# First feed-forward of a decoder block: four plain tiles in place of six, chunks of 6, 8 and 8

## The chip, the cores and the metric

The kernel runs on one core of a Trainium2 chip (trn2). The metric is the device time of one execution in microseconds (us). Five engines work side by side, each through its own queue in order: PE (TensorE, matrix products; PEld its weight loads), DVE (VectorE), ACT (ScalarE), POOL (GpSimd) and SP (SyncE, which issues nearly all transfers).

## What is computed

One decoder block on 528 tokens (16 learned meta tokens ahead of 512) with 1024 channels, in fp32: a SwiGLU feed-forward, a token mixer (latent attention beside a gated DeltaNet), a second SwiGLU feed-forward, a final norm. The change touches the first feed-forward alone:

```python
def swiglu(x, w_gate, w_up, w_down):
    return (jax.nn.silu(x @ w_gate) * (x @ w_up)) @ w_down

h = h + 0.5 * swiglu(rmsnorm(h, ffn1_norm[l]), ffn1_w_gate[l], ffn1_w_up[l], ffn1_w_down[l])
```

`w_gate` and `w_up` are 1024 x 2816, `w_down` is 2816 x 1024. The hidden size of 2816 is 22 tiles of 128.

## The kernel before, in words

Activations lie with channels on the 128 partitions and tokens along the row: `hk`, eight tiles of 128 x 528. Each fp32 product is made of three fast ones: an operand is split into a rounded high part (ACT casts it) and the remainder (DVE subtracts), and high x high, high x low and low x high are added up in PSUM. So each weight tile costs a cast on ACT and a subtraction on DVE before PE can use it.

A feed-forward is the function `ffn`, called for both. Its 22 hidden tiles `ft` go in chunks (`CHUNKS1`, `CHUNKS2`). The first `2 * nc_` tiles are **plain** (`NC1 = 3` in the first feed-forward, `NC2 = 2` in the second): for gate and for up, `weights` loads and splits a 128 x 1024 weight (L175 to L177), `mm3` (L204) runs 8 x 3 x 2 matmuls of 264 columns, the result is multiplied by the norm's `r` (L390; for the first two tiles L376 and L386), and gate and up are joined (L400). Such a product (gate or up of one tile) is called a unit here: six plain tiles are twelve units of 48 matmuls.

The other tiles go by twos through `quad` (L440), a scheme of Strassen and Winograd on a 2 x 2 split of weights, channels and tokens: 7 products instead of 8. Each product is 12 matmuls of 264 columns, so a quad is 84, and two tiles take two quads (gate, up). In exchange DVE and ACT have more to do: in a quad, DVE makes four sums of weights (`side`, L429, tiles `sf`), the low halves of seven weight forms (`form`, L292; ACT casts the high halves, L291) and seven sums of results from PSUM (L433); ACT copies one result (L456). DVE joins the two tiles at L495.

A quad also needs the activations in another form, which DVE and ACT build once per feed-forward while PE is busy with the plain tiles: for each of four pairs of `hk` tiles two scalings by `r` (L407), four differences (L413) and splits (L291, L292) into tiles `hd` (named `b`, `yh`, `yl` in the code) and `ut` (`sh`, `sl`, `th`, `tl`). The scaling needs `r`, thus the norm of the whole input.

When a chunk's tiles are done, each is split (`halve`, L292 `hd<-hd,ra`), and `down` (L204 `dn`, L345) multiplies the chunk by eight blocks of `w_down`; these eight calls are spread over the quads of the chunk behind it, and the last chunk's eight stand at the end. A `down` of 8 tiles is 48 matmuls, of 6 tiles 36.

```python
for ft in range(2 * nc_):                       # plain tiles
for c, (k0, k1) in enumerate(CHUNKS):
    nq = max(k1 - max(k0, 2 * nc_), 0)
    for ft in range(max(k0, 2 * nc_), k1, 2):
        for j in range(2):
            quad(ft, j, *os)
            if c:
                while given < KT * q // nq:
                    down(c - 1, given)
    for ft in range(k0, k1):
        halve(ft)
for m in range(KT):
    down(len(CHUNKS) - 1, m)
```

The order on each engine is not this program order: a scheduler sorts the instructions when the program is built, and each engine then takes its own queue strictly as it stands. The weight tiles rotate through a few buffers, and the forms through three kinds in turn (`CYCLE`, counted over both feed-forwards).

Of the kernel before, what the change touches and what calls it, by code (L numbers as in the profile page):

```python
# [51 lines left out]
M34 = 17.5  # L52
WLO = ()
LAG = 3
NC1 = 3
NC2 = 2
CHUNKS1 = ((0, 8), (8, 16), (16, 22))
CHUNKS2 = ((0, 6), (6, 14), (14, 22))
BANKS = "smastsa"
NG = 3  # L60
# [35 lines left out]
def build(tc, a, out, tap=None):  # L96
# [3 lines left out]
    with ctx:  # L100
# [202 lines left out]
        def ffn(wg, wd, xs, hks, wname, r, n, hid, tmp, ra, rb, hk_tile, nc_, load, finish, pre=()):  # L303
            raws, hs, hkm = [], {}, {}
            pre = list(pre)
            h = n // 2
            CHUNKS = CHUNKS1 if n == NT else CHUNKS2

# [201 lines left out]
        with tc.tile_pool(name="hid", bufs=1) as hid, tc.tile_pool(name="fp", bufs=2) as fp:  # L510
# [61 lines left out]

            ffn(a["w1"], a["d1"], xs, hks, "n1", r, NT, hid, fp, ra1, upt, hk1, NC1, load1, finish1, pre)
            r = norm2.finish(D, "r")
# [984 lines left out]
```

## Time and profile before

| | |
|---|---|
| median of 3 runs | 1169.24 us (1168.03 to 1169.33) |
| profiled execution | 1168.86 us, its span 1167.1 us |
| PE busy | 1152.7 us, 99% of the span |
| DVE busy | 859.5 us, 74% |
| ACT busy | 560.3 us, 48% |
| chain that ended last | PE 94%; DVE 2%; ACT 2%; DMA 1% |
| granted TensorE clock, mean | 0.998 of full speed |

The profile is of one execution; times in it count from the start of its span. A row of the timeline shows the start, the time from the first start to the last end in it, the engine, the line, the operation and the tiles. Rows of one engine overlap a little, since an instruction begins before the one ahead of it has written its last value: the pace of a queue is the distance from start to start, not the duration. This holds for PE above all, where a matmul of 264 columns is shown with 0.28 us and the next one starts 0.12 us after it.

### The profile page before, as it was taken

To read this page: it belongs to the slowest core of one execution; us is meant where nothing else is said; L and a number is where in the kernel's file an instruction comes from. 1 tells how busy PE (TensorE), PEld (TensorE's weight loads), DVE (VectorE), ACT (ScalarE), POOL (GpSimd) and SP (SyncE) were. 2 spreads that over 40 slices of the span, in tenths; PEclk is the share of its full clock that TensorE was granted. 3 is DMA by queue.
4 is the path that set the end of the run, shared out by engine and by line. 5 is a ranking of instruction groups with operands and counts; after the bars stand their busy time and mean duration, and the time that the engine had idled before them with its cause. 6 is when DMAs were issued, how large, how long until landed. Compare 5 with 4: busy or idle time off the path is not lost.

```text
span 1167.1 us, 20801 instructions
## 1 busy us (share of the span) xinstructions
PE 1152.7 (99%) x8132; PEld 1053.9 (90%) x8132; DVE 859.5 (74%) x1588; ACT 560.3 (48%) x989; POOL 83.0 (7%) x108
## 2 busy tenths in 40 slices
PE   9999999999999999999999999999999999999997
PEld 9999999999999989888877888878899999999986
DVE  6998787776665879963786666645999878877744
ACT  7554343533445584365466554434454445433443
POOL 0000000000003221001100000221000000000011
PEclk9999999999999999999999999999999999999999
DMA  6432332333235433445656445555433333323322
GB/s 243 129 124 96 109 104 97 95 94 103 82 101 174 153 89 122 138 148 154 186 157 180 136 131 167 184 178 174 155 105 132 111 93 105 101 100 107 93 71 73
DMA packets 74114, 148.51 MB, mean 127 GB/s; under 512 B 20288, under 2 KB 30864, under 8 KB 74016
## 3 DMA queue, kind: packets, MB, share of 16 engines
q1 hardware_dynamic: 73472, 146.66, 39.9%
q8 instruction: 64, 1.05, 0.4%
q10 hardware_dynamic: 544, 0.52, 0.1%
q14 instruction: 34, 0.28, 0.1%
HBM read 128.56 MB, written 18.60 MB: 126 GB/s over the span
## 4 chain that ended last, share of the span: by engine, by line
PE 94%; DVE 2%; ACT 2%; DMA 1%; issue 1%; SPq 0%; DVEq 0%; ACTq 0%
PE gu L440 30%; PE dn L204 21%; PE gu L204 10%; PE gate L204 8%; PE wo L204 4%; PE mo L204 4%; PE qkv L204 3%; PE z L204 2%; PE s L1169 2%; PE cq L204 1%; ACT dec L150 1%; PE pt L1202 1%; PE o L1231 1%; PE qk L1025 1%; PE vn L996 1%; PE qn L204 1%
## 5 line engine op out<-in xcount | busy, mean ns | idle before, releaser
L176 ACT CAST whi<-wraw 128x1024 fp32r<-128x1024 f32 (+2 forms) x121 | 122.9, 1016 | 174.1 <-issue 66.4
L177 DVE TENSOR_TENSOR wlo<-wraw,whi 128x1024 fp32r<-128x1024 f32 (+2 forms) x121 | 146.5, 1211 | 24.6 <-ACT whi L176 24.4
L440 PE MATMUL gu<-hd,form 128*128 128x256 f32 (+1 forms) x1224 | 164.7, 283 | 0.0
L440 PEld LDWEIGHTS gu<-hd,form 128*128 128x128 f32 x1224 | 155.9, 190 | 1.6
L291 ACT CAST form<-sf 128x512 fp32r<-128x512 f32 x136 | 83.0, 620 | 113.9 <-DVE sf L429 65.7
L440 PE MATMUL gu<-rb,form 128*128 128x256 f32 x864 | 112.6, 283 | 0.0
L345 DVE SCALAR_TENSOR_TENSOR hk<-dn,hk 128x528 f32<-128x528 f32 (+2 forms) x50 | 33.9, 678 | 100.7 <-PE dn L204 100.7
L440 PEld LDWEIGHTS gu<-rb,form 128*128 128x128 f32 x864 | 107.7, 192 | 0.0
L291 ACT CAST form<-wraw 128x512 fp32r<-128x512 f32 x102 | 63.1, 620 | 85.9 <-PE gu L440 56.4
L292 DVE TENSOR_TENSOR form<-sf,form 128x512 fp32r<-128x512 f32 x136 | 92.8, 688 | 12.3 <-ACT form L291 12.1
L440 PE MATMUL gu<-ut,form 128*128 128x264 f32 x768 | 101.1, 284 | 0.0
L204 PE MATMUL dn<-hd,whi 128*128 128x264 f32 (+2 forms) x376 | 99.0, 315 | 0.0
L440 PEld LDWEIGHTS gu<-ut,form 128*128 128x128 f32 x768 | 96.5, 188 | 0.0
L204 PE MATMUL gate<-ut,whi 128*128 128x512 f32 x256 | 86.5, 412 | 1.3 <-DVE gt L1259 1.3
L204 PE MATMUL dn<-ut,whi 128*128 128x512 f32 (+1 forms) x248 | 85.4, 381 | 0.0
L204 PE MATMUL dn<-ra,whi 128*128 128x264 f32 x464 | 85.3, 285 | 0.0
L292 DVE TENSOR_TENSOR form<-wraw,form 128x512 fp32r<-128x512 f32 x102 | 69.8, 687 | 6.4 <-ACT form L291 6.0
L204 PE MATMUL dn<-ut,wlo 128*128 128x512 f32 (+1 forms) x192 | 72.1, 375 | 0.0
L204 PE MATMUL dn<-ra,wlo 128*128 128x264 f32 x352 | 71.6, 285 | 0.0
L204 PEld LDWEIGHTS dn<-ra,whi 128*128 128x128 f32 x464 | 68.5, 189 | 0.0
L204 PEld LDWEIGHTS dn<-hd,whi 128*128 128x128 f32 x376 | 62.9, 189 | 3.9
L204 PE MATMUL qkv<-ut,whi 128*128 128x264 f32 x384 | 65.2, 288 | 0.0
(434 smaller groups left out, 2311.5 us busy)
## 6 DMA issues: line engine op xcount, KB each, us to landing
wraw<-w SPq DMA_DIRECT2D x86, 512.0 KB, 3.3
wraw<-win SPq DMA_DIRECT2D x36, 512.0 KB, 3.5
wraw<-d SPq DMA_DIRECT2D x32, 512.0 KB, 3.7
wraw<-d SPq DMA_DIRECT2D x16, 384.0 KB, 3.2
hk<-xT SPq DMA_DIRECT2D x16, 264.0 KB, 4.4
dec<-growd SPq DMA_DIRECT2D x8, 512.0 KB, 6.2
gated<-gt SPq DMA_DIRECT2D x16, 256.0 KB, 2.0
sg<-gated SPq DMA_DIRECT2D x16, 256.0 KB, 2.9
```

Of the source, the lines that this page charges most:

```text
L150: ins = nc.scalar.activation(*args, **kw).ins
L176: ih = nc.scalar.copy(hi[:, 0:n], raw[:, 0:n])
L177: il = (nc.gpsimd if pool_lo else nc.vector).tensor_tensor(out=lo[:, 0:n], in0=raw[:, 0:n], in1=hi[:, 0:n].bitcast(F32), op=ALU.subtract)
L204: trail.append(nc.tensor.matmul(o, lhsT=w, rhs=x[:, lo_:hi_], start=start and k == 0 and pi == 0, stop=stop and k == n - 1 and pi == 2).ins)
L291: nc.scalar.copy(hi, x)
L292: (eng or nc.vector).tensor_tensor(out=lo, in0=x, in1=hi.bitcast(F32), op=ALU.subtract)
L345: nc.vector.scalar_tensor_tensor(out=o, in0=p, scalar=0.5, in1=o, op0=ALU.mult, op1=ALU.add)
L440: nc.tensor.matmul(ps, lhsT=wt, rhs=xt, start=k == 0 and i == 0, stop=k == 3 and i == 2)
L996: nc.tensor.matmul(psv[:, h], lhsT=X[c][:, h], rhs=rr[:, h], start=True, stop=True)
L1025: nc.tensor.matmul(ps[:, h4], lhsT=hs(kT, h, o, o + n), rhs=hs(qT, h, o, o + n), start=True, stop=True)
L1169: nc.tensor.matmul(ps[:, 0:w], lhsT=Q[h][:, b * P:(b + 1) * P], rhs=K[h][:, k0:k1], start=True, stop=True)
L1202: nc.tensor.transpose(out=ps[:, b * P:(b + 1) * P], in_=Pr[h // 2, b][:, h % 2, NM + c * P:NM + (c + 1) * P], identity=ident)
```

## The change

The first feed-forward takes the numbers that the second one has: four plain tiles in place of six, and chunks of 6, 8 and 8 tiles in place of 8, 8 and 6.

```diff
-NC1 = 3
+NC1 = 2
 NC2 = 2
-CHUNKS1 = ((0, 8), (8, 16), (16, 22))
+CHUNKS1 = ((0, 6), (6, 14), (14, 22))
 CHUNKS2 = ((0, 6), (6, 14), (14, 22))
```

So tiles 4 and 5 go through two quads in place of four units; chunk 0 has four plain tiles and two quads (before: six and two), chunk 1 has eight quads, now with calls of `down` of 6 tiles between them (before: 8), chunk 2 has eight quads (before: six) with calls of 8 tiles (as before), and the eight calls at the end have 8 tiles (before: 6).

What the queues look like is shown at three places, as rows of line, operation, output, inputs and shape; numbers behind a name tell buffers apart.

**DVE, at the third plain tile's end.** The two queues are the same up to the first row here. `wlo` is the low part of a plain unit's weight, `hk` and `hd`, `ut` the activations for the quads. Before:

```order
L400 TENSOR_TENSOR hd_455<-g_454,hd_455 128x528
L177 TENSOR_TENSOR wlo_691<-wraw_689,whi_690 128x1024
L413 TENSOR_TENSOR hk_110<-hk_110 128x264
L407 SCALAR_TENSOR_TENSOR hk_111<-hk_111,cols_74,r_213 128x528
L413 TENSOR_TENSOR hk_110<-hk_114,hk_110 128x264
L407 SCALAR_TENSOR_TENSOR hk_115<-hk_115,cols_74,r_213 128x528
L413 TENSOR_TENSOR hk_114<-hk_114,hk_110 128x264
L292 TENSOR_TENSOR ut_953<-hk_110,ut_952 128x528
L390 TENSOR_TENSOR g_570<-gu_572,r_213 128x528
L413 TENSOR_TENSOR hk_114<-hk_114 128x264
L177 TENSOR_TENSOR wlo_748<-wraw_746,whi_747 128x1024
```

With the change:

```order
L400 TENSOR_TENSOR hd_455<-g_454,hd_455 128x528
L413 TENSOR_TENSOR hk_110<-hk_110 128x264
L407 SCALAR_TENSOR_TENSOR hk_111<-hk_111,cols_74,r_213 128x528
L413 TENSOR_TENSOR hk_110<-hk_114,hk_110 128x264
L407 SCALAR_TENSOR_TENSOR hk_115<-hk_115,cols_74,r_213 128x528
L413 TENSOR_TENSOR hk_114<-hk_114,hk_110 128x264
L292 TENSOR_TENSOR ut_721<-hk_110,ut_720 128x528
L413 TENSOR_TENSOR hk_114<-hk_114 128x264
L292 TENSOR_TENSOR hd_730<-hk_111,hd_730 128x264
L292 TENSOR_TENSOR hd_732<-hk_115,hd_731 128x528
L390 TENSOR_TENSOR g_570<-gu_572,r_213 128x528
L292 TENSOR_TENSOR ut_723<-hk_114,ut_722 128x528
```

The weight splits `wlo` of tiles 4 and 5 (691, 748 and two more) have gone from the queue, and with them the results of these tiles; what is left moves up.

**DVE, the first weight forms.** The last rows of the activations and the forms of the first quad. Before:

```order
L292 TENSOR_TENSOR ut_995<-hk_112,ut_994 128x528
L413 TENSOR_TENSOR hk_116<-hk_116 128x264
L429 TENSOR_TENSOR sf_1031<-sf_1029,wraw_1006 128x512
L429 TENSOR_TENSOR sf_1067<-wraw_1006,wraw_1007 128x512
L292 TENSOR_TENSOR ut_997<-hk_116,ut_996 128x528
L390 TENSOR_TENSOR hd_687<-gu_745,r_213 128x528
L292 TENSOR_TENSOR form_1013<-wraw_1006,form_1013 128x512
L400 TENSOR_TENSOR hd_687<-g_686,hd_687 128x528
L292 TENSOR_TENSOR form_1034<-sf_1031,form_1034 128x512
```

With the change:

```order
L400 TENSOR_TENSOR hd_571<-g_570,hd_571 128x528
L413 TENSOR_TENSOR hk_112<-hk_112 128x264
L292 TENSOR_TENSOR form_781<-wraw_774,form_781 128x512
L413 TENSOR_TENSOR hk_112<-hk_116,hk_112 128x264
L429 TENSOR_TENSOR sf_797<-wraw_775 128x512
L413 TENSOR_TENSOR hk_116<-hk_116,hk_112 128x264
L292 TENSOR_TENSOR ut_763<-hk_112,ut_762 128x528
L413 TENSOR_TENSOR hk_116<-hk_116 128x264
L429 TENSOR_TENSOR sf_799<-sf_797,wraw_774 128x512
L292 TENSOR_TENSOR form_819<-wraw_774,form_819 128x512
L292 TENSOR_TENSOR ut_765<-hk_116,ut_764 128x528
L292 TENSOR_TENSOR form_802<-sf_799,form_802 128x512
```

Before, `form_1013` (the first quad's first product) stands behind `hd_687`, the result of the tenth of twelve units; now `form_781` (the same product) stands right behind `hd_571`, the result of the eighth and last unit, and `form_819` and `form_802` (its third and second product) follow.

**PE, from the last plain unit to the first quad.** `gu` are the PSUM tiles; the first row is the last plain matmul pair. Before:

```order
L204 MATMUL gu_861<-ra_171,wlo_864 128x264 x2
L440 MATMUL gu_1012<-hd_920,form_1013 128x264 x3
L440 MATMUL gu_1012<-hd_941,form_1013 128x264 x3
L440 MATMUL gu_1012<-hd_962,form_1013 128x264 x3
L440 MATMUL gu_1012<-hd_983,form_1013 128x264 x3
L440 MATMUL gu_1033<-ut_933,form_1034 128x264
```

With the change:

```order
L204 MATMUL gu_629<-ra_171,wlo_632 128x264 x2
L440 MATMUL gu_780<-hd_688,form_781 128x264 x2
L440 MATMUL gu_818<-hd_689,form_819 128x264
L440 MATMUL gu_818<-hd_690,form_819 128x264
L440 MATMUL gu_780<-hd_688,form_781 128x264
L440 MATMUL gu_780<-hd_709,form_781 128x264 x3
L440 MATMUL gu_780<-hd_730,form_781 128x264 x3
L440 MATMUL gu_780<-hd_751,form_781 128x264 x3
L440 MATMUL gu_818<-hd_689,form_819 128x264
L440 MATMUL gu_801<-ut_701,form_802 128x264
L440 MATMUL gu_801<-ut_702,form_802 128x264
L440 MATMUL gu_818<-hd_710,form_819 128x264
```

Before, a product's twelve matmuls stand together. Now two matmuls of the third product (`gu_818`) are put between the second and the third one of the first product (`gu_780`); the third matmul of each is the first that reads the low half of its form.

**DVE, the first forms of chunk 1.** The splits of chunk 0's tiles (`hd<-hd,ra`), the joins of its last two tiles (L495), and the forms of chunk 1's first quad: `form_1321`, `form_1342`, `form_1359` before, `form_1081`, `form_1119` with the change. Before:

```order
L292 TENSOR_TENSOR hd_1295<-hd_687,ra_1294 128x528
L429 TENSOR_TENSOR sf_1337<-wraw_1315 128x512
L292 TENSOR_TENSOR hd_1299<-hd_803,ra_1298 128x528
L429 TENSOR_TENSOR sf_1339<-sf_1337,wraw_1314 128x512
L433 TENSOR_TENSOR cp_1146<-gu_1169,p1_1147 128x264
L292 TENSOR_TENSOR form_1359<-wraw_1314,form_1359 128x512
L292 TENSOR_TENSOR form_1321<-wraw_1314,form_1321 128x512
L433 TENSOR_TENSOR hd_1004<-gu_1186,p1_1147 128x264
L292 TENSOR_TENSOR form_1342<-sf_1339,form_1342 128x512
```

With the change:

```order
L292 TENSOR_TENSOR hd_1055<-hd_455,ra_1054 128x528
L433 TENSOR_TENSOR hd_772<-gu_1010,cp_914 128x264
L292 TENSOR_TENSOR hd_1059<-hd_571,ra_1058 128x528
L495 TENSOR_TENSOR hd_772<-hd_772,g_770 128x528
L433 TENSOR_TENSOR hd_773<-gu_1027,cp_914 128x264
L292 TENSOR_TENSOR form_1081<-wraw_1074,form_1081 128x512
L495 TENSOR_TENSOR hd_773<-hd_773,g_771 128x528
L292 TENSOR_TENSOR hd_1063<-hd_772,ra_1062 128x528
L429 TENSOR_TENSOR sf_1097<-wraw_1075 128x512
L292 TENSOR_TENSOR hd_1067<-hd_773,ra_1066 128x528
L429 TENSOR_TENSOR sf_1099<-sf_1097,wraw_1074 128x512
L292 TENSOR_TENSOR form_1119<-wraw_1074,form_1119 128x512
```

Before, three forms of this quad stand ahead of the joins (which come 11 rows below the last row shown) and of the splits of the last two tiles; now `form_1081` stands behind a join and the last splits of plain tiles, and `form_1119` behind both joins and all six splits.

## Rows read from the trace of the kernel before

**Rows 1.** The page, part 1: busy time, share of the span, instructions.

```profile
PE 1152.7 (99%) x8132; PEld 1053.9 (90%) x8132; DVE 859.5 (74%) x1588; ACT 560.3 (48%) x989; POOL 83.0 (7%) x108
```

**Rows 2.** Waits of PE over the whole span: total us, times, longest.

```profile
PE gu L204 <- ACT whi L190: 1.3, 1, 1.3
```

**Rows 3.** Windows of the first feed-forward: busy time by engine, clock, DMA.

```profile
core 0: us, PE busy (x) PEld busy (x) DVE busy (x) ACT busy (x) POOL busy (x), PEclk, DMA share, GB/s
...
78.13:108.73 30.60, 30.60 (x255) 30.60 (x253) 30.38 (x58) 16.00 (x29) 0.00 (x0) 1.00 0.33 104
108.73:205.17 96.44, 96.44 (x795) 96.44 (x793) 73.06 (x130) 38.34 (x62) 0.00 (x0) 1.00 0.31 99
```

**Rows 4.** Timeline of PE: start, us, operation, count in the row.

```profile
54.98 0.65 PE L204 MATMUL gu<-ra,whi 128*128 128x264 f32 x4
...
78.13 1.62 PE L440 MATMUL gu<-hd,form 128*128 128x264 f32 x12
...
108.73 0.40 PE L204 MATMUL dn<-ra,whi 128*128 128x264 f32 x2
```

**Rows 5.** Timeline of DVE, norm and first rows behind it.

```profile
29.42 0.43 DVE L225 SCALAR_TENSOR_TENSOR r<-rsq,r 128x264 f32<-128x264 f32 x1
...
35.87 1.45 DVE L407 SCALAR_TENSOR_TENSOR hk<-hk,cols,r 128x528 f32<-128x528 f32 x2
...
45.48 0.71 DVE L400 TENSOR_TENSOR hd<-g,hd 128x528 f32<-128x528 f32 x1
```

**Rows 6.** Timeline of DVE, consecutive rows, for the pace of each kind.

```profile
54.26 0.78 DVE L407 SCALAR_TENSOR_TENSOR hk<-hk,cols,r 128x528 f32<-128x528 f32 x1
54.94 0.45 DVE L413 TENSOR_TENSOR hk<-hk 128x264 f32<-128x264 f32 x1
...
61.22 0.45 DVE L413 TENSOR_TENSOR hk<-hk 128x264 f32<-128x264 f32 x1
61.56 0.71 DVE L292 TENSOR_TENSOR form<-wraw,form 128x512 fp32r<-128x512 f32 x1
62.16 0.72 DVE L390 TENSOR_TENSOR g<-gu,r 128x528 f32<-128x528 f32 x1
62.78 1.24 DVE L177 TENSOR_TENSOR wlo<-wraw,whi 128x1024 fp32r<-128x1024 f32 x1
63.91 0.45 DVE L413 TENSOR_TENSOR hk<-hk 128x264 f32<-128x264 f32 x1
...
68.60 0.71 DVE L292 TENSOR_TENSOR form<-wraw,form 128x512 fp32r<-128x512 f32 x1
...
106.45 0.43 DVE L433 TENSOR_TENSOR cp<-gu,cp 128x264 f32<-128x264 f32 x1
106.79 0.69 DVE L429 TENSOR_TENSOR sf<-sf,wraw 128x512 f32<-128x512 f32 x1
```

**Rows 7.** Timeline of DVE in the second feed-forward: first scaling, first forms.

```profile
816.05 0.75 DVE L407 SCALAR_TENSOR_TENSOR hk<-hk,cols,r 128x512 f32<-128x512 f32 x1
...
842.91 0.69 DVE L292 TENSOR_TENSOR form<-wraw,form 128x512 fp32r<-128x512 f32 x1
...
848.16 0.69 DVE L292 TENSOR_TENSOR form<-sf,form 128x512 fp32r<-128x512 f32 x1
```

**Rows 8.** Timeline of PE in the second feed-forward: first product of its first quad.

```profile
850.75 1.59 PE L440 MATMUL gu<-hd,form 128*128 128x256 f32 x12
```

**Rows 9.** Windows at the end of the span, columns as in rows 3.

```profile
1158.50:1159.00 0.50, 0.12 (x1) 0.00 (x0) 0.00 (x0) 0.34 (x1) 0.00 (x0) 1.00 0.00 0
...
1161.50:1162.00 0.50, 0.00 (x0) 0.00 (x0) 0.50 (x2) 0.00 (x0) 0.00 (x0) 0.72 0.00 0
1162.00:1162.50 0.50, 0.00 (x0) 0.00 (x0) 0.50 (x2) 0.00 (x0) 0.00 (x0) 0.50 0.00 0
```

**Rows 10.** Timeline of DVE in the last calls of `down`, first feed-forward.

```profile
348.70 0.71 DVE L345 SCALAR_TENSOR_TENSOR hk<-dn,hk 128x528 f32<-128x528 f32 x1 [2.08 <-PE dn L204]
349.37 0.96 DVE L177 TENSOR_TENSOR wlo<-wraw,whi 128x768 fp32r<-128x768 f32 x1
```

## The prediction

> **What bounds the kernel now.** I read the page first, then the waits, then windows and timelines of the first feed-forward. PE is busy for 99% of the span [rows 1], and in the whole span the longest wait of PE is one of 1.3 us, at the start [rows 2]. So PE's own queue is the time: each matmul less counts, as long as the other engines keep ahead, and each wait that a change brings to PE counts in full. The reader should then look at how far ahead DVE is. While the two quads of chunk 0 and the first of chunk 1 run, DVE is busy for 30.38 of 30.60 us; with the calls of `down` between the quads, for 73.06 of 96.44 us [rows 3]. So DVE has no spare time just at the stretch that the change makes earlier.
>
> **The gain on PE.** Four plain units, 192 matmuls, take from 54.98 to 78.13 us, 23.15 us; three quads, 252 matmuls, take 30.60 us up to 108.73 us, 10.20 us each or 0.1214 us a matmul [rows 4]. Tiles 4 and 5 go from four units to two quads: 20.40 − 23.15 = **−2.75 us**.
>
> **What comes earlier.** PE is done with the eighth unit at 54.98 us [rows 4]. Up to there its queue is the same as before. Before, it then had four more units, and DVE and ACT had these 23 us for the activations and the first forms. Now the first quad follows at once. The activations can't start earlier: the last half of `r` is written from 29.42 us on, and the first scaling starts at 35.87 us [rows 5].
>
> **DVE's queue, counted out.** The paces, start to start [rows 6]: a scaling L407 0.68 us; a difference or split of 264 columns 0.34; a form or weight sum of 512 columns 0.60; an operation on 528 columns 0.62; a `wlo` 1.13; a sum from PSUM (L433) 0.34. Up to L400 at 45.48 us [rows 5] the two queues are the same, so the next row starts at 46.10. Between it and `form_781` there now stand 24 rows: 11 of 264 columns (3.74), 4 scalings (2.72), 9 of 528 columns (5.58), together 12.04 us. The result of the eighth unit is among them; PE has it by 55.3, DVE comes to it at about 55.9, so DVE does not wait there. `form_781` starts at 58.14 and ends 0.71 us later [rows 6], at 58.85.
>
> - **First wait.** PE issues four matmuls (54.98 to 55.47) and stands at the first that reads the low half of `form_781`: 58.85 − 55.47 = 3.38 us. Ten matmuls follow (1.21), to 60.06.
> - **Second wait.** `form_819` starts seven rows behind `form_781` (3 × 0.60 + 3 × 0.34 + 0.62 = 3.44), at 61.58, and ends at 62.29: 2.23 us. `form_802` starts at 61.58 + 0.60 + 0.62 = 62.80 and ends at 63.51, ten matmuls later, just when PE needs it.
> - **Third and fourth wait.** From `form_802` to `form_1081` there are 37 rows: 18 of 512 columns (10.80), 14 sums (4.76), 5 of 528 (3.10), 18.66 us. So `form_1081` starts at 81.46 and ends at 82.17. PE has 154 matmuls of the two quads left at 62.29 (18.70) and four of the third: 81.48. Wait 0.69 us; ten matmuls, 83.38. `form_1119` starts six rows on (0.60 × 3 + 0.62 × 3 = 3.66) at 85.12 and ends at 85.83: wait 2.45 us.
>
> Together 3.38 + 2.23 + 0.69 + 2.45 = **+8.75 us**. Behind that the rest of this quad (8.5 us) reads forms that DVE makes at 0.60 us each, and the first `down` gives DVE 4.3 us of PE time for one `wlo` and one sum.
>
> **The other edits, at nothing.** ACT casts 28 half forms in place of 4 weights; it is busy for 16.00 of 30.60 us there [rows 3], and each cast it owes DVE stands one or more rows ahead. The transfers are the same in number and size; SP now issues the eight reloads of `hk` ahead of chunk 1's first weights, but they wait for the same DVE rows as the first quad from about 63 us on, and have some 15 us until `form_1081`. In chunk 1 a quad with a `down` of 6 tiles gives PE 10.20 + 36 × 0.1206 = 14.5 us, and DVE needs what it needs now, 73.06/6 = 12.2 us for each of six quads with a `down` [rows 3], less the shorter `wlo`: cover 2.3 us a quad. If it went, each of eight quads would wait. The last eight calls have 2.08 us of idle DVE time each [rows 10], and now more PE time; the eight tiles of the last chunk are split while `down` of chunk 1 still runs. The 14 forms more shift the rotation of form buffers in the second feed-forward by 126 − 112 = 14, two places of three; a few of its DVE rows trade places, by one row of 0.60 us or less, where the forms are some 7 us ahead of PE [rows 7, 8]: taken as nothing, with half a microsecond either way.
>
> **Sum.** 8.75 − 2.75 = +6.0 us. The profiled execution has 1168.86 us, so 1174.9 us; its median is 0.4 us higher, and I say **1175.0 us**. For the waits the counted queue leaves DVE no idle time, so below 8 us they would have to run at a pace that no row shows; above, a late cast here and there may add 1 to 2 us. The forecast's own range is 1173.5 to 1177.5.
>
> [...]
>
> **The rivals.**
> [...]
> 2. *DVE keeps ahead and the gain stays.* For it: the second feed-forward has these very numbers and PE never waits in it [rows 2]. Its first scaling starts at 816.05, the first form at 842.91 and the third at 848.16 [rows 7], and PE begins its quad at 850.75 [rows 8], 34.7 us behind the first scaling. Against it: here that distance is 54.98 − 35.87 = 19.1 us, and the first form came 26.9 us behind the scaling there; here three `wlo` and two results fewer (4.6 us) lie between, which leaves 22.3 us, as counted. It decides at a total wait of 2.75 us: the forms would have to come 3 us sooner and chunk 0's splits to leave the way. Then 1168.86 − 2.75 = 1166.1 us.
> 3. *Only part of the waits comes*, as when the two around chunk 0's splits and half of the first are hidden: 8.75 − 0.69 − 2.45 − 1.69 = 3.9 us, net +1.2: 1170.1 us.
> 4. *DVE stays behind all through chunk 1.* For it: 12 of 14.5 us is little slack for a queue in order. Against it: the second feed-forward's chunk 1 has calls of 6 tiles too, without a wait [rows 2]. At 1 us in each of eight quads: 1183 us.
> 5. *The change does not do what it says*: the queues above show 24 matmuls fewer and the quads in place, so this has no share.
>
> **How the numbers follow.** Forecast 0.72, rival 1 0.13, rival 2 0.05, rival 3 0.06, rival 4 0.04. A measurement of this kernel can tell about 0.2%, 2.3 us, from no change. Faster by more than that: rival 2, 0.05. Within it: rival 3, 0.06. Slower: 0.89. The range takes in the forecast's own, rival 1 with a margin of a microsecond, and the upper half of rival 3's way: 1171.5 to 1178.5.
>
> **What would show it.** In the new profile: waits of PE on DVE `form` (line 292) at 55 to 62 us and at 81 to 86 us, the first the longest, some 8 to 9 us in all; the first `dn` at about 94.4 us (108.73 before); DVE without idle time from 46 to 88 us; PE without waits from there on, and a second feed-forward as long as before. The forecast is wrong if PE goes from the eighth unit into the quad without a gap, or if the waits are there and the time is not longer: then something behind them has become shorter. A granted clock below 1.00 between 55 and 66 us speaks for rival 1, waits in each quad of chunk 1 for rival 4.

## The result, and the profile after

The changed kernel takes 1177.94 us (median of 4 runs, 1177.6 to 1178.8), the kernel before, run beside it, 1169.28 us (4 runs, 1168.03 to 1169.63). The ratio is 1.0079, with a 95% interval of 1.0065 to 1.0093: **8.7 us slower**. The profiled execution of the changed kernel has 1177.6 us and a span of 1175.8 us, 8.7 us more than that of before.

The page of the changed kernel, part 1, against [rows 1]:

```profile
PE 1154.9 (98%) x8108; PEld 1054.6 (90%) x8108; DVE 869.1 (74%) x1616; ACT 563.9 (48%) x1001; POOL 85.1 (7%) x108
```

PE has 24 matmuls fewer and yet 2.2 us more busy time. So some matmuls seem to have become slower; the sum of the prediction has no term for that. Then the waits of PE, where [rows 2] had nothing above 1.3 us:

```profile
PE gu L440 <- DVE form L292: 7.4, 3, 3.3
...
PE gu L440 <- DVE hd L433: 0.6, 1, 0.6
```

Four waits, 8.0 us. The timeline of PE (start, us, operation, count, idle time just before and who ended it) shows where they stand, against [rows 4]:

```profile
54.08 0.65 PE L440 MATMUL gu<-hd,form 128*128 128x264 f32 x4
58.01 1.48 PE L440 MATMUL gu<-hd,form 128*128 128x264 f32 x10 [3.28 <-DVE form L292]
61.47 0.59 PE L440 MATMUL gu<-hd,form 128*128 128x264 f32 x1 [1.98 <-DVE form L292]
...
66.47 3.14 PE L440 MATMUL gu<-ut,form 128*128 128x264 f32 x24
...
83.59 2.08 PE L440 MATMUL gu<-hd,form 128*128 128x264 f32 x12 [0.57 <-DVE hd L433]
87.85 0.39 PE L440 MATMUL gu<-hd,form 128*128 128x264 f32 x1 [2.18 <-DVE form L292]
...
96.48 0.41 PE L204 MATMUL dn<-ra,whi 128*128 128x264 f32 x2
```

These are the four waits of the prediction, in its four places. Only the third is not quite as forecast: PE waits first for a sum from PSUM (L433), which stands just ahead of `form_1081` in DVE's queue, and two matmuls later for that form. This second part lies inside the row at 83.59, which takes 2.08 us for twelve matmuls where [rows 4] have 1.62. PE enters the first quad at 54.08, where before it was at its ninth plain unit at 54.98 [rows 4]; that 0.90 us is an earlier start of the whole execution (one such wait at the start is missing here, that of [rows 2]).

The windows of the same stretch (length, busy time and count for each engine, granted clock of PE, DMA share, GB/s) show what makes the matmuls slow:

```profile
58.01:59.50 1.49, 1.48 (x10) 1.27 (x10) 1.49 (x4) 0.63 (x1) 0.00 (x0) 1.00 0.33 128
59.50:61.47 1.97, 0.01 (x1) 0.01 (x1) 1.97 (x5) 1.61 (x4) 0.00 (x0) 0.56 0.22 44
61.47:62.29 0.82, 0.82 (x3) 0.82 (x4) 0.82 (x2) 0.82 (x2) 0.00 (x0) 0.50 0.60 224
...
66.03:66.47 0.44, 0.44 (x3) 0.44 (x3) 0.20 (x1) 0.00 (x0) 0.00 (x0) 0.50 0.00 0
66.47:67.50 1.03, 1.03 (x10) 1.03 (x10) 1.02 (x3) 0.00 (x0) 0.00 (x0) 0.95 0.00 0
...
82.61:87.85 5.24, 2.40 (x17) 1.76 (x15) 5.24 (x10) 2.27 (x5) 0.00 (x0) 1.00 0.01 3
87.85:96.48 8.63, 8.63 (x71) 8.63 (x72) 8.60 (x17) 4.71 (x8) 0.00 (x0) 1.00 0.45 134
```

Behind the first wait ten matmuls run at the full clock (1.00). Early in the second wait the clock falls (0.99 from 59.50 to 59.75 us, 0.50 from 59.75 to 61.47), and it is at 0.50 until about 66.5. In the two later waits and behind them it stays at 1.00 (82.61 to 96.48 us). The 22 matmuls from 61.47 to 66.47 take 5.00 us where 22 × 0.1214 = 2.67 us are the pace of [rows 4]: **+2.33 us**.

DVE, in the same stretch (idle time in brackets):

```profile
57.27 0.69 DVE L292 TENSOR_TENSOR form<-wraw,form 128x512 fp32r<-128x512 f32 x1
...
60.73 0.68 DVE L292 TENSOR_TENSOR form<-wraw,form 128x512 fp32r<-128x512 f32 x1
...
66.27 0.43 DVE L433 TENSOR_TENSOR cp<-gu,p 128x264 f32<-128x264 f32 x1 [1.83 <-PE gu L440]
...
83.45 0.68 DVE L292 TENSOR_TENSOR form<-wraw,form 128x512 fp32r<-128x512 f32 x1
...
87.11 0.68 DVE L292 TENSOR_TENSOR form<-wraw,form 128x512 fp32r<-128x512 f32 x1
```

These are the four forms that the prediction counted to, at 58.14, 61.58, 81.46 and 85.12. Less the 0.89 us of the earlier start (the row behind L400 begins at 45.21 here, at 46.10 in the count) the first two were to come at 57.25 and 60.69: they come at 57.27 and 60.73. The other two come 2.88 us late. The reader should see the row at 66.27: while PE is slow, DVE runs out of work, and stands for 1.83 us; the rest of the 2.88 us is made of smaller gaps, such as one of 0.27 us behind PE at 75.93.

**Where the 8.7 us come from.** In front of the first `down`, before, there were four plain units and three quads (54.98 to 108.73, 53.75 us). Now there are three quads (54.08 to 96.48, 42.40 us), and two more quads come later, at 20.40 us by the pace of [rows 4]: 62.80 us, which is 9.05 more. The earlier start takes 0.90 off. From the first `down` to the first matmul of the mixer it is 282.70 us (96.48 to 379.18) against 261.77 (108.73 to 370.50), 0.53 more than the two quads. From there to the first quad of the second feed-forward, 0.43 more; behind that, 0.41 less. Together 8.70 us. So nearly everything lies ahead of the first `down`.

### The profile page after: what moved, and what is told of

It is laid out like the page before. It is cut to its first block, busy times and chain, and to the rows that moved or that the text cites. A ratio compares the mean times of both kernels' runs of the same rounds, so it can differ in the third digit from the quotient of the medians.

```text
span 1175.8 us, 20796 instructions
## 1 busy us (share of the span) xinstructions
PE 1154.9 (98%) x8108; PEld 1054.6 (90%) x8108; DVE 869.1 (74%) x1616; ACT 563.9 (48%) x1001; POOL 85.1 (7%) x108
## 4 chain that ended last, share of the span: by engine, by line
PE 90%; DVE 6%; ACT 2%; issue 1%; DVEq 0%; ACTq 0%
PE gu L440 31%; PE dn L204 21%; PE gate L204 8%; PE gu L204 5%; PE wo L204 4%; PE mo L204 4%; PE qkv L204 3%; PE z L204 2%; PE s L1169 2%; PE cq L204 1%; ACT dec L150 1%; PE pt L1202 1%; PE o L1231 1%; DVE wlo L177 1%; PE qk L1025 1%
## 5 line engine op out<-in xcount | busy, mean ns | idle before, releaser
L176 ACT CAST whi<-wraw 128x1024 fp32r<-128x1024 f32 (+2 forms) x117 | 118.7, 1015 | 162.1 <-issue 66.5
L440 PE MATMUL gu<-hd,form 128*128 128x264 f32 (+1 forms) x1296 | 177.3, 285 | 8.1 <-DVE form L292 7.4
L440 PEld LDWEIGHTS gu<-hd,form 128*128 128x128 f32 x1296 | 166.6, 191 | 10.8 <-DVE form L292 8.4
L177 DVE TENSOR_TENSOR wlo<-wraw,whi 128x1024 fp32r<-128x1024 f32 (+2 forms) x117 | 139.7, 1194 | 21.1 <-ACT whi L176 20.4
L291 ACT CAST form<-sf 128x512 fp32r<-128x512 f32 x144 | 87.4, 620 | 122.5 <-DVE sf L429 81.2
L440 PE MATMUL gu<-ut,form 128*128 128x264 f32 x864 | 116.2, 286 | 0.0
L440 PEld LDWEIGHTS gu<-ut,form 128*128 128x128 f32 x864 | 110.7, 190 | 0.0
L292 DVE TENSOR_TENSOR form<-sf,form 128x512 fp32r<-128x512 f32 x144 | 97.6, 684 | 13.9 <-ACT form L291 13.3
L291 ACT CAST form<-wraw 128x512 fp32r<-128x512 f32 x108 | 66.6, 621 | 84.4 <-PE gu L440 55.4
L292 DVE TENSOR_TENSOR form<-wraw,form 128x512 fp32r<-128x512 f32 x108 | 73.9, 685 | 7.6 <-ACT form L291 7.2
```

What stands on the lines that cost most here:

```text
L176: ih = nc.scalar.copy(hi[:, 0:n], raw[:, 0:n])
L177: il = (nc.gpsimd if pool_lo else nc.vector).tensor_tensor(out=lo[:, 0:n], in0=raw[:, 0:n], in1=hi[:, 0:n].bitcast(F32), op=ALU.subtract)
L291: nc.scalar.copy(hi, x)
L292: (eng or nc.vector).tensor_tensor(out=lo, in0=x, in1=hi.bitcast(F32), op=ALU.subtract)
L440: nc.tensor.matmul(ps, lhsT=wt, rhs=xt, start=k == 0 and i == 0, stop=k == 3 and i == 2)
```

## The experiments

The theory after the result: DVE owes PE the forms when the quads come 23 us earlier, because four plain units were the cover in which it made up for its queue; the waits that follow drop the clock (0.50 from 59.75 to about 66.5 us), which has a price of its own. The rivals: the new chunks cost; the clock takes only time that DVE owes anyway; PE waits for something other than DVE's queue.

Each kernel was timed beside the kernel before, whose median there lay between 1168.80 and 1169.49 us. So a difference of less than about 1 us between two changed kernels is not told by their medians; where it matters, the difference of their distances from the kernel before is given too.

### The two parts of the change, one at a time

```diff
-NC1 = 2
+NC1 = 3
```

> Chunks of 6, 8 and 8 tiles, but still six plain tiles. Theory (DVE owes forms because the quads start 23 us earlier; the chunks have no part in it): no wait of PE on a form above 1 us in the first feed-forward, the plain units end near 78 us as before, clock 1.00 there, time as before, 1168 to 1171 us. Rival (the early split of chunk 0 and the calls of down behind it are what costs): waits of PE of 4 us or more between 78 and 110 us, 1173 us or more.

Measured: 1169.21 us against 1168.80, ratio 1.0004 (0.9995 to 1.0013). No wait on a form; in the timeline of PE the quad follows the plain units at once, and `down` follows the quad:

```profile
78.06 1.62 PE L440 MATMUL gu<-hd,form 128*128 128x264 f32 x12
...
88.29 0.40 PE L204 MATMUL dn<-ra,whi 128*128 128x264 f32 x2
```

```diff
-CHUNKS1 = ((0, 6), (6, 14), (14, 22))
+CHUNKS1 = ((0, 8), (8, 16), (16, 22))
```

> Four plain tiles, but the chunks of before (8, 8 and 6 tiles). Theory: the first two waits on forms stay as in the changed kernel, 3.3 and 2.0 us between 55 and 62 us, with the clock at about 0.5 from the second of them until some 66 us; the two later waits move behind the third and fourth quad or become one; 1175 to 1179 us. Rival (the chunks cost): the gain of 2.75 us shows, less a wait or two of under 1 us, 1166 to 1168 us.

Measured: 1179.07 us, just above what was expected, ratio 1.0087 (1.0073 to 1.0101); the gain alone would give 0.9976. The waits in its timeline of PE:

```profile
58.52 1.48 PE L440 MATMUL gu<-hd,form 128*128 128x264 f32 x10 [3.27 <-DVE form L292]
61.97 0.59 PE L440 MATMUL gu<-hd,form 128*128 128x264 f32 x1 [1.98 <-DVE form L292]
...
104.61 0.51 PE L440 MATMUL gu<-hd,form 128*128 128x264 f32 x2 [0.57 <-DVE hd L433]
107.06 4.39 PE L440 MATMUL gu<-hd,form 128*128 128x264 f32 x20 [1.94 <-DVE form L292]
```

The first two waits stay where they were. The other two move some 20 us back with the end of chunk 0. Behind the last of them matmuls are slow a second time here: the twenty in the row at 107.06 take 4.39 us, where 20 × 0.1214 = 2.43 are the pace of [rows 4]. That is enough for a time above that of the changed kernel. So the loss comes with the plain tiles, and the chunks only say where the second pair of waits stands: behind the splits of chunk 0.

### Keeping PE at work in the waits

```diff
+            if n == NT:
+                idle, low = tk_tile("idle"), xf[1][3][1]
+                for _ in range(28):
+                    nc.tensor.matmul(idle[:, 0:h], lhsT=low[:, 0:P], rhs=low, start=True, stop=True)
```

> The changed kernel with 28 more matmuls of 264 columns, whose result is not used, between the eighth plain unit and the first quad (28 x 0.1214 = 3.40 us, as long as the first wait). Theory (the low clock behind the waits costs 2.4 us of its own): PE is busy where it waited 3.3 us, the second wait of 2.0 us stays, the clock is 1.00 from 48 to 72 us, the 22 matmuls behind the second wait take 0.12 us each, 1175 to 1176 us. First rival (the low clock costs nothing, since DVE owes the time anyway): 1177.5 to 1178.5 us with the clock at 1.00. Second rival (the second wait alone drops the clock): the clock falls all the same, 1177.5 us or more.

Measured: 1177.33 us (1176.89 to 1177.4), 0.6 us less than the changed kernel (0.1 by the distances from the kernel before, 8.53 and 8.66): no gain that can be told, and not the 2 us expected. Its timeline of PE, then two of its windows:

```profile
54.77 3.63 PE L425 MATMUL idle<-hd 128*128 128x264 f32 x28 [0.34 <-DVE hd L292]
...
61.65 0.39 PE L445 MATMUL gu<-hd,form 128*128 128x264 f32 x1 [1.54 <-DVE form L292]
...
81.50 2.08 PE L445 MATMUL gu<-hd,form 128*128 128x264 f32 x12 [0.57 <-DVE hd L438]
85.76 0.39 PE L445 MATMUL gu<-hd,form 128*128 128x264 f32 x1 [2.19 <-DVE form L292]
```

```profile
61.65:64.45 2.80, 2.80 (x23) 2.80 (x23) 2.80 (x5) 1.98 (x4) 0.00 (x0) 1.00 0.55 160
...
85.76:89.88 4.12, 4.12 (x23) 4.12 (x24) 3.25 (x6) 3.07 (x6) 0.00 (x0) 0.64 0.15 24
```

In the first place the theory holds: clock 1.00, and the same 22 matmuls take 2.80 us, not 5.00 (the second wait is shorter here too, 1.54 us for 1.98). PE is at its third wait 2.09 us earlier (81.50 for 83.59), and that wait and the next have kept their length, so this time was not owed by DVE. But now the clock falls behind the fourth wait, where it had stayed at 1.00 in the changed kernel: 22 matmuls take 4.12 us there, against 2.78 (87.85 to 90.63). Of 2.20 us gained 1.34 are given back. The expectation missed since it held the second place for safe. That is what the next run tests:

```diff
+                    if n == NT and ft == 6:
+                        idle = tk_tile("idle")
+                        for _ in range(23):
+                            nc.tensor.matmul(idle[:, 0:h], lhsT=low[:, 0:P], rhs=low, start=True, stop=True)
                     for j in range(2):
                         os = (gs, raws[-2:])[j]
                         quad(ft, j, *os)
```

> As the run that fills the first wait, and 23 more unused matmuls (2.79 us) between the second quad and the first quad of chunk 1, where 0.57 and 2.19 us of waits stood. Theory (the low clock is a cost of its own, paid once in each of the two places unless PE keeps working): clock 1.00 from 48 to 100 us, the first matmul of down 2.1 us earlier than in the changed kernel's 96.48, at 94.0 to 94.8 us, 1175.2 to 1176.3 us. Rival (what the clock takes DVE owes anyway): the first down at 95.5 us or later, 1177 us or more.

Measured: 1176.0 us (1175.71 to 1176.84), 1.9 us less than the changed kernel (1.5 by the distances from the kernel before, 7.18 and 8.66), as expected. Timeline of PE:

```profile
55.17 3.67 PE L425 MATMUL idle<-hd 128*128 128x264 f32 x28 [0.35 <-DVE hd L292]
...
62.05 0.39 PE L445 MATMUL gu<-hd,form 128*128 128x264 f32 x1 [1.49 <-DVE form L292]
...
80.93 2.93 PE L496 MATMUL idle<-hd 128*128 128x264 f32 x23
...
86.17 0.39 PE L445 MATMUL gu<-hd,form 128*128 128x264 f32 x1 [0.60 <-DVE form L292]
...
94.82 0.41 PE L204 MATMUL dn<-ra,whi 128*128 128x264 f32 x2
```

One window each, from the end of the last plain matmul to the first `down`, of this kernel (first) and of the changed one (second):

```profile
54.82:94.82 40.00, 37.55 (x304) 37.13 (x304) 39.67 (x76) 19.03 (x34) 0.00 (x0) 1.00 0.34 104
```

```profile
54.24:96.48 42.24, 34.15 (x254) 33.09 (x253) 39.91 (x76) 19.12 (x34) 0.00 (x0) 0.92 0.32 100
```

The same 76 rows of DVE; with the clock at 1.00 DVE stands for 0.33 us (40.00 − 39.67), with the clock at 0.92 for 2.33 (42.24 − 39.91). So the price of the low clock is 2 us or a little more, and the stretch without it is as long as DVE's rows. 51 matmuls more make the kernel faster.

### DVE's debt: more of it, and less

```diff
+            if n == NT:
+                spare = hid.tile([P, 4, P], F32, tag="sf", name="spare", bufs=NSF)
+                for _ in range(4):
+                    nc.vector.tensor_tensor(out=spare, in0=r[:, 0:512].rearrange("p (a b) -> p a b", a=4), in1=r[:, 0:512].rearrange("p (a b) -> p a b", a=4), op=ALU.add)
```

The same edit in the changed kernel and in the one before:

> The changed kernel with four more rows of 512 columns on DVE (4 x 0.60 = 2.4 us, result not used) ahead of the first form. Theory (DVE owes the time): the waits at 54 to 64 us grow by 2.4 us together, from 5.3 to about 7.7 us, and the time by 2.0 to 3.0 us: 1179.5 to 1181.5 us. Rival (DVE's idle 1.8 us behind the slow matmuls, or another wait, takes it up): 1177.5 to 1178.5 us.

> The kernel before with the same four rows (2.4 us) of DVE at the same place of the program. Theory (there the four plain units are the cover): no wait of PE above 0.5 us at 55 to 110 us, same time, 1168.3 to 1170 us. Rival (DVE is as late in the kernel before, only unseen): 2 us or more slower, 1171 us.

Measured: in the kernel before 1168.63 us, ratio 0.9998 (0.9989 to 1.0007), nothing. Its first form is made at 69.28 us (61.56 in [rows 6]; that is more than the dose, since the scheduler also put other rows ahead of it), and PE, which comes to it at 77.57, still does not wait:

```profile
69.28 0.68 DVE L292 TENSOR_TENSOR form<-wraw,form 128x512 fp32r<-128x512 f32 x1
```

In the changed kernel 1178.34 us (1177.34 to 1179.89), 0.4 us more (0.9 by the distances from the kernel before), not 2 to 3. The two first waits have become one, of 6.74 us in place of 5.26:

```profile
61.73 4.33 PE L445 MATMUL gu<-hd,form 128*128 128x264 f32 x17 [6.74 <-DVE form L292]
...
97.72 0.41 PE L204 MATMUL dn<-ra,whi 128*128 128x264 f32 x2
```

```profile
54.50:97.72 43.22, 34.29 (x253) 33.50 (x252) 41.96 (x79) 18.53 (x33) 0.00 (x0) 0.88 0.33 99
```

The expectation missed, and the rival has a share. To the first `down` DVE is busy for 2.05 us more than in the changed kernel (79 rows, 76 + 4 − 1), but idle for 1.26 us where that was 2.33: the stretch grows by 0.98 us. DVE's idle time behind the slow matmuls takes up about half of the dose. The profiled execution, 1179.89 us, is the longest of the five, so its rows rather overstate what the dose costs.

Then the debt made smaller. The first attempt moved three of the `wlo` of the plain units to POOL, which does nothing there (the third argument sends the subtraction to POOL):

```diff
-                return pre.pop(0) if pre else weights(wg[ft, j], KT)
+                return pre.pop(0) if pre else weights(wg[ft, j], KT, n == NT and 2 * ft + j >= 5)
```

> The changed kernel, with the low parts of the weights of the last three plain units subtracted on POOL, not on DVE: DVE is spared 3 x 1.13 = 3.4 us before its first form. Theory (the waits are what DVE owes): the first wait shrinks from 3.3 us to nothing or up to 1 us, the second stays at about 2 us or takes a part of it, the clock stays at 1.00 or falls later; waits of 4 to 5 us in all, 1171.5 to 1174.5 us. Rival (the waits hang on something other than DVE's queue, such as casts of ACT or results of PE): the first wait stays near 3.3 us, 1177 to 1178.5 us.

Measured: 1180.76 us, ratio 1.0101 (1.0087 to 1.0115), slower than the changed kernel. The timelines of POOL and of DVE:

```profile
30.01 2.92 POOL L177 TENSOR_TENSOR wlo<-wraw,whi 128x1024 fp32r<-128x1024 f32 x1 [28.69 <-ACT whi L176]
35.20 2.40 POOL L177 TENSOR_TENSOR wlo<-wraw,whi 128x1024 fp32r<-128x1024 f32 x1 [2.27 <-ACT whi L176]
42.80 5.08 POOL L177 TENSOR_TENSOR wlo<-wraw,whi 128x1024 fp32r<-128x1024 f32 x1 [5.21 <-PE gu L204]
```

```profile
30.59 2.90 DVE L386 TENSOR_TENSOR g<-g,r 128x528 f32<-128x528 f32 x1
...
45.56 2.90 DVE L407 SCALAR_TENSOR_TENSOR hk<-hk,cols,r 128x528 f32<-128x528 f32 x1
```

The DVE row at 30.59 takes 0.70 us in the changed kernel; here it ends 0.56 us after POOL's row (33.49 and 32.93). The rows at 35.34 (2.82 for 0.76) and 45.56 (2.90 for 0.76) end 0.56 and 0.58 us after POOL's second and third row: 6.4 us more in three rows, to spare 3 × 1.13 = 3.4 us. So DVE's debt grew by some 3 us, and PE had three long waits, of 2.3, 3.7 and 2.2 us (the second ends with ACT's cast of a form, at 64.33, of a sum that DVE made only at 63.50). Not every DVE row beside a row of POOL is long: POOL's third runs from 42.80 to 47.88, the DVE rows that start from 43.01 to 45.21 keep their usual length (0.69, 1.04 for two together, 0.69 and 0.42 us), and the long one overlaps only the last 2.3 us of it. What ties the two engines is not shown here. As a test of the theory the run is void: it was meant to take work off DVE and did the opposite. The second attempt leaves work out:

```diff
-                split(tmp, x, sh, sl)
-                split(tmp, y, th, tl)
+                nc.scalar.copy(sh, x)
+                nc.scalar.copy(th, y)
+                sl, tl = sh, th
```

(in the first feed-forward only)

> The changed kernel without the eight subtractions that make the low parts of the differences and sums of the activations (the tiles ut, 8 x 0.62 = 4.96 us of DVE; their high parts are read in their place, so products 4 to 7 of the first feed-forward are computed from wrong low parts). PE's work is the same. Theory (DVE owes the time): the first two waits, 5.26 us, go to 0.5 us or less, the clock stays at 1.00 up to 80 us, the two later waits stay at 2 to 2.8 us; 1170.5 to 1172.5 us. Rival (what PE waits for hangs on ACT's casts or on transfers): the first two waits keep 2 us or more, 1174 us or more.

Measured: 1170.78 us (11 runs) against 1169.12, ratio 1.0012 (1.0002 to 1.0022), 7 us less than the changed kernel for 4.96 us of DVE. The profiled execution, 1173.71 us, is the longest of the eleven. Its timeline of PE:

```profile
56.85 1.37 PE L445 MATMUL gu<-ut,form 128*128 128x264 f32 x9 [0.40 <-DVE form L292]
...
76.72 2.08 PE L445 MATMUL gu<-hd,form 128*128 128x264 f32 x12 [0.47 <-DVE hd L438]
...
80.98 0.39 PE L445 MATMUL gu<-hd,form 128*128 128x264 f32 x1 [2.18 <-DVE form L292]
```

Of the 5.26 us of the first two waits 0.40 are left; the other two stay, as expected. That more comes back than DVE was spared is the clock again: it is at 1.00 from 54 to 78 us in the windows of this run. Behind the last wait it falls in the profiled execution (0.50 from 82 to 84 us; the 22 matmuls from 80.98 to 85.28 take 4.30 us); whether it falls in the median one too, no trace here shows. ACT's work is as before, and in the changed kernel ACT itself stood for 2.24 us, up to 57.10, waiting for DVE. So the first waits do not hang on its casts.

### Keeping half of the gain

If two plain units are cover enough, one of the two quads of the tiles 4 and 5 can stay:

```diff
                     for j in range(2):
                         os = (gs, raws[-2:])[j]
-                        quad(ft, j, *os)
+                        if not (n == NT and ft == 4 and j):
+                            quad(ft, j, *os)
```

with the two up units computed as plain ones just ahead of it.

> The changed kernel, but of the tiles 4 and 5 only the gate goes as a quad; their two up units stay plain, ahead of that quad. Theory (plain units are the cover in which DVE makes up its 5.6 us): the two plain units are 11.6 us of cover, so no wait of PE on a form above 0.5 us between 55 and 100 us, clock 1.00 there, and half of the 2.75 us stays as a gain: 1.4 us less than the kernel before in the same call, 1167.2 to 1168.2 us. Rival (quads so early are held up by something that two units do not cover): waits of 1.4 us or more remain, 1169 us or more.

Measured: 1171.98 us, ratio 1.0029 (1.0018 to 1.0041). The plain units wait now, for their own low parts, which stand behind the preparation of the activations in DVE's queue:

```profile
58.71 0.81 PE L204 MATMUL gu<-ra,wlo 128*128 128x264 f32 x2 [1.86 <-DVE wlo L177]
```

The clock is at 0.50 behind it (window 60 to 62 us). So the place in the queue matters, not only the sum. With the two units ahead of that preparation in the program, the rest of the edit being the same:

```diff
+            for ft in range(4, 6) if n == NT else ():
+                raws.append(raw_tile(ft)[:, 0:n])
+                ps = mm_tile("gu")
+                mm3(outs528(ps), gate_up(ft, 1), xs, True, True)
+                nc.vector.tensor_tensor(out=v2(raws[ft]), in0=halves(ps), in1=v2(r), op=ALU.mult)
+
             lhs, rhs = slice(0, h), slice(h, n)
```

> As the run with half of the pair, but the two plain up units stand in the program with the other eight, ahead of the preparation of the activations, so that their low parts come early in DVE's queue (there PE waited 1.86 us for one of them, and the clock fell behind it). Theory (two plain units are 11.6 us of cover for 5.6 us that DVE owes): no wait of PE above 0.5 us from 48 to 100 us, clock 1.00 there, 1.4 us less than the kernel before in the same call: 1167.1 to 1168.1 us. Rival (half a pair is not to be had without a wait): waits of 1.4 us or more together, 1169 us or more.

Measured: 1168.22 us (11 runs) against 1169.12, ratio 0.9997 (0.9988 to 1.0006): the loss is gone, a gain can't be told. The profiled execution, 1171.92 us, is the longest of the eleven, but hardly by its first feed-forward: there the clock is at 1.00 (in each window up to 100 us), while the page has it at 8 tenths in the slice from 556 to 585 us, in the token mixer. One wait is left, in the first quad of chunk 1:

```profile
81.93 2.70 PE L446 MATMUL gu<-ut,form 128*128 128x264 f32 x20 [0.80 <-DVE form L292]
```

Two rows of DVE ahead of that form split the tiles 4 and 5, which only the next `down` reads. They go behind the quad, and in a second step one of the two products of gate and up with them:

```diff
+                        if n == NT and c == 1 and q == 1:
+                            for t in range(4, k0):
+                                halve(t)
...
-                for ft in range(k0, k1):
+                for ft in range(k0, 4 if n == NT and c == 0 else k1):
                     halve(ft)
```

> As the run with the up units first, and the splits of the tiles 4 and 5 stand behind the first quad of chunk 1, not ahead of it: two rows of DVE (1.24 us) leave the way of the form for which PE still waited 0.80 us. Theory: no wait of PE above 0.3 us from 48 to 100 us, the whole half of the gain of a pair, 1.4 us less than the kernel before in the same call: 1167.4 to 1168.0 us where that has 1169.1. Rival (the wait moves to the first down, which reads these splits): a wait of 0.8 us or more at its matmuls, 1168.2 us or more.

> As the run with the late splits, and the second of the two products of gate and up (0.62 us of DVE) also stands behind the form for which PE still waited 0.40 us. Theory: that wait is gone, no wait of PE on a form above 0.1 us from 48 to 100 us, 1.2 to 1.4 us less than the kernel before in the same call: 1167.3 to 1167.8 us where that has 1168.8. Rival (the form waits for something else, a cast or a transfer): the wait of 0.4 us stays, about 0.9 us less than before, 1167.9 us.

Measured: 1167.95 us against 1168.82, ratio 0.9992 (0.9983 to 1.0001), and 1168.37 against 1169.49, ratio 0.9991 (0.9982 to 1.0000), 11 runs each. The wait in the timeline of PE of the second, and rows of its timeline of DVE:

```profile
81.26 2.95 PE L446 MATMUL gu<-ut,form 128*128 128x264 f32 x22 [0.41 <-DVE form L292]
```

```profile
79.52 0.74 DVE L508 TENSOR_TENSOR hd<-hd,g 128x528 f32<-128x528 f32 x1
80.14 0.46 DVE L439 TENSOR_TENSOR cp<-gu,p 128x264 f32<-128x264 f32 x1
80.48 0.72 DVE L292 TENSOR_TENSOR form<-sf,form 128x512 fp32r<-128x512 f32 x1
```

The late splits halved the wait (0.40 us, where at most 0.3 was expected); it did not move to the first `down`. The late product did not touch it, against the expectation, and the rows of DVE show why: L508 is that product, and the scheduler left it ahead of the form that PE waits for (80.48). So the step was not done, and what it is worth is not shown. Both kernels come out 0.9 and 1.1 us under the kernel before, which is 1.38 less 0.40; the intervals end at 1.0001 and 1.0000, so the gain is likely, less than the 1.2 to 1.4 us expected, and just not shown by either alone.

## Why the prediction was wrong in its size

**The direction and the waits were right.** The gain of 2.75 us on PE agrees with what could be seen of it: one half, 1.38 less a wait of 0.40, with the 0.9 to 1.1 us of the last two runs. The four waits came in their places; rivals 2, 3 and 4 did not come, and the chunks, the casts and the second feed-forward cost nothing that can be measured, as said (the run with the chunks alone; 0.43 us up to the second feed-forward).

**The count of DVE's queue was right** to 0.04 us for the two first forms; the two others came 2.88 us late. From start to start, as the prediction counts, the waits are 3.44 (54.57 to 58.01), 2.25 (59.22 to 61.47), 1.20 (82.85 to 83.59, and 2.08 − 1.62 = 0.46 inside the row behind it) and 2.34 us (85.51 to 87.85), together 9.23 for 8.75. (The brackets of the timeline show less, 8.01, since a row's idle time begins where the modelled end of its last matmul lies, and a gap inside a row has no bracket.)

**What failed is a term that the sum does not have, the clock's.** 8.75 − 2.75 sets it at nothing, on the view that the first wait would be over about when the clock fell at the end of the span before, some 3 us behind the last matmul (0.72 from 1161.5 to 1162.0 us, 0.50 behind that [rows 9]). That comparison holds for the first wait: the ten matmuls behind it ran at 1.00. It left out that 1.2 us later the second wait follows. The clock fell there (0.50 from 59.75 us on), and the 22 matmuls behind it took 2.33 us more. In the sum: 8.75 + 0.48 (the waits as measured) + 2.33 − 2.75 = 8.8 us, against 8.7 measured. That it comes out so close is partly luck: the earlier start (−0.90) happens to take off what small additions, of 0.24 us up to the first `down` and of 0.55 behind it, put on. Two signs that the prediction names show it: the first `down` came at 96.48, which is 97.38 in the times of before, where 94.4 was forecast, and DVE did not stay without idle time. Rival 1 is the forecast with a low clock behind the first wait, at an estimate of 2.4 us: by the 0.50 of [rows 9] 22 matmuls take twice as long, 2.7 us more, less a part that DVE owes anyway; together 1177.4 us. In the run the 22 took 5.00 us at 0.50, where the pace of [rows 4] gives 2.67. So this rival describes what happened but for the place of the fall, and 1177.94 us lies at its side, above the forecast's own range.

**The part that DVE owes anyway was wrong too.** DVE had rows to do while PE was slow, so part of the price seemed to be owed. But behind the slow matmuls DVE waits for PE in turn (1.83 us at 66.27), and its later forms come later, by 2.88 us at the third. So the two later waits kept at least their length (3.54 us, 3.14 forecast), and the price came on top. The run with PE kept at work in both places shows the same: DVE's idle time in the stretch goes from 2.33 to 0.33 us, and the time falls by 1.5 to 1.9 us.

## What to carry to other kernels

Work that a change takes out of PE's queue may have been the cover in which another engine made up its own: count that engine's queue from the last point at which both kernels are the same, row by row. Where such a count gives waits, price the clock behind them as a term of its own (2.33 us here), and look at all waits near each other, not at the longest alone. Half of a change may keep part of a gain that the whole of it loses, if the half that stays leaves the cover standing (here some 1 us, at the edge of what can be told).

## What the runs showed of the hardware that was not expected

- A wait of about 2.2 us at the full clock was followed by the low level in some executions and not in others: not at 87.85 in the changed kernel (1.00 over the next 8.63 us), but at 85.76 in the run with the first wait filled (0.64 over the next 4.12 us), for the same rows and the same wait, at 80.98 in the run without the low parts (0.50 from 82 to 84 us), and, by the pace, behind 1.94 us at 107.06 in the run with the plain tiles alone (20 matmuls in 4.39 us for 2.43). The length of one wait did not decide it; what does is open here. Profiles are of one execution each, so the medians may hold both.
- Matmuls whose result nobody reads made a kernel faster: 51 of them took 1.5 to 1.9 us off, with the clock at 1.00 from the last plain matmul to the first `down` where it was 0.92.
- With three subtractions on POOL, one DVE row beside each took 2.8 to 2.9 us in place of 0.70 or 0.76 and ended 0.56 to 0.58 us after it; other DVE rows beside the third kept their length.
